# One ring, one list: replacing groups and pools by a single ordered list of operations for all engines

## Chip, cores, metric

One core of one Trainium2 chip, the other cores idle. The time is device microseconds of one execution. The profile's span is shorter than the time reported, by 1.7 to 2.2 us (3.0 and 2.9 in two executions of run 14). Engines: PE multiplies matrices, DVE is the vector engine, ACT the one for Ln and Exp, POOL is GpSimd; SBUF is the on-chip memory that holds the rows, PSUM the one that PE writes, in banks. All runs quoted are of the fast state; ratios are the mean time of one kernel's fast runs over that of the kernel before in the same rounds on the same chip, so not quite the ratio of the medians quoted. The kernel before was 174.5 to 175.4 us by chip and round.

## The reference

```python
x = np.abs(np.random.randn(32, 512, 1024)).astype(np.float32) + 1e-6
return np.sum(1.0 / x, axis=-1).astype(np.float32)
```

16384 rows of 1024 numbers lie as 128 partitions of 128 rows; "row" below means one row on all 128 partitions, 0.524 MB. There is no divide: with a and b the two halves of a row, 1/a + 1/b = (a + b) / (ab). So a product ab (512 wide), Ln, Exp(-x) for 1/(ab), and a multiply with a sum over the row.

## The kernel before

```python
A, B, C = (2, 0, GP, False), (2, 0, GP, True), (1, 1, GP, False)
GROUPS = ([A, B, A, B, C, B, A, B] * 7 + [A, B, A, B, A]
          + [(1, 0, GP, True), (1, 0, GP, False)] * 2 + [(1, 0, GP, True), (1, 0, DV, True)])
# xpool 16 buffers, ppool 4, rpool and spool (PSUM) 2 each
for np_, ns, eng, on_pe in GROUPS:
    xt = xpool.tile([P, n, D], f32, tag="xt")
    nc.sync.dma_start(out=xt, in_=x_v[:, c0 : c0 + n, :])        # mostly 2 rows, 1 MB
    eng.tensor_tensor(out=pr, in0=xt[:, :np_, :H], in1=xt[:, :np_, H:], op=mult)  # POOL
    if on_pe:   # a + b on PE: two matmuls with the identity into one PSUM bank
        for j in range(np_):
            for h in range(2):
                nc.tensor.matmul(sm[:, j, :], lhsT=ident, rhs=xt[:, j, h*H:(h+1)*H],
                                 start=h == 0, stop=h == 1)
    ...  # 7 rows go through ACT alone: Ln, Exp over the whole row
    nc.scalar.activation(out=pr, in_=pr, func=Ln, scale=S)
    nc.scalar.activation(out=rc, in_=pr, func=Exp, scale=-1.0)   # rc = pr, or PSUM
    ...  # DVE: "short" reduction rc * sm (512 wide), or "long" xt * rc (1024 wide)
```

## Time and profile before

| | before | changed |
|---|---|---|
| time, us | 174.56 | 179.68 |
| span of the profiled run | 172.6 | 177.8 |
| loads | 67 | 34 |
| last load landed | 164.0 | 162.5 |
| last reduction ended | 169.8 | 175.2 |
| busy: PE / DVE / ACT / POOL | 121 / 110 / 142 / 143 | 148 / 139 / 131 / 117 |

Landing minus start is transfer; last reduction minus last landing is what the engines still owe when the input is complete. The views are in the prediction.

### The profile page before, as it was taken

Reading aid. Unit: us, or ns where it says so; the run is one execution under the profiler, and the core shown is the slowest. Engines: PE = TensorE matmul, PEld = TensorE weight load, DVE = VectorE, ACT = ScalarE, POOL = GpSimd, SP = SyncE. Lnnn points to the kernel's source line nnn. Section 1 sums busy time; section 2 is a strip of 40 time slices with the busy share of each in tenths; the row PEclk is TensorE's granted clock in tenths of the full one; section 3 lists DMA queues with packets and bytes.
Section 4 is the critical chain, followed back from the end, with each engine's and each line's share of the span. In section 5 each row is a group of like instructions: output and inputs, shape, how many; then the busy total and the mean of one; then the engine's idle time right before and its main releaser. Section 6 shows DMA issues by size and latency. Waiting matters only on the chain.

```text
span 172.6 us, 1342 instructions
## 1 busy us (share of the span) xinstructions
PE 120.9 (70%) x256; PEld 47.4 (27%) x256; DVE 109.8 (64%) x243; ACT 142.0 (82%) x156; POOL 143.4 (83%) x72
## 2 busy tenths in 40 slices
PE   0099776767876767788666668977667876669480
PEld 0043322222332222233322223422222332223130
DVE  0009757874776757775578847468576755787791
ACT  2159989899878998889888996889988898988981
POOL 1599699969989799987999688997999979999920
PEclk9999999999999999999999996999999999999999
DMA  5999999999999999999999999999999999999500
GB/s 190 416 433 425 423 420 423 421 421 423 418 425 420 423 418 423 423 420 423 421 421 420 423 414 423 421 420 420 425 418 425 425 420 421 421 412 408 220 0 15
DMA packets 9799, 67.25 MB, mean 390 GB/s; under 512 B 1088, under 2 KB 1216, under 8 KB 1984
## 3 DMA queue, kind: packets, MB, share of 16 engines
q1 hardware_dynamic: 9792, 67.18, 94.0%
q8 instruction: 2, 0.03, 0.1%
q14 instruction: 5, 0.04, 0.1%
HBM read 67.11 MB, written 0.07 MB: 389 GB/s over the span
## 4 chain that ended last, share of the span: by engine, by line
DMA 78%; POOL 11%; ACT 2%; issue 2%; DVE 2%; SPq 1%; PE 1%; POOLq 0%; DVEq 0%
DMA xt<-in_x_dram 78%; POOL pr L85 11%; SPq L83 1%; ACT pr L106 1%; PE sm L90 1%; DVE xt L118 1%; ACT rc L111 1%; DVE pr L118 0%; ACT pr L111 0%; DVE pr L85 0%; POOLq L85 0%; DVE sums L118 0%; DVEq L118 0%; DVEq L157 0%
## 5 line engine op out<-in xcount | busy, mean ns | idle before, releaser
L85 POOL TENSOR_TENSOR pr<-xt 128x1024 f32<-128x1024 f32 (+1 forms) x66 | 142.7, 2166 | 21.1 <-DMA xt<-in_x_dram 15.2
L90 PE MATMUL sm<-xt,ident 128*128 128x512 f32 x256 | 120.9, 617 | 47.0 <-DMA xt<-in_x_dram 45.0
L118 DVE CUSTOM_DVE_ANT_1 xt<-xt,rc 128x1024 f32<-128x1024 f32 x57 | 67.7, 1219 | 50.2 <-issue 27.2
L106 ACT ACTIVATE pr<-pr 128x1024 f32<-128x1024 f32 (+1 forms) x67 | 65.0, 970 | 24.5 <-POOL pr L85 23.7
L90 PEld LDWEIGHTS sm<-xt,ident 128*128 128x128 f32 x256 | 47.4, 195 | 119.7 <-issue 57.8
L118 DVE CUSTOM_DVE_ANT_0 pr<-pr,sm 128x512 f32<-128x512 f32 x64 | 41.6, 685 | 9.8 <-ACT pr L111 8.6
L111 ACT ACTIVATE pr<-pr 128x1024 f32<-128x1024 f32 (+1 forms) x34 | 34.2, 1006 | 1.0
L111 ACT ACTIVATE rc<-pr 128x1024 f32<-128x1024 f32 (+1 forms) x33 | 29.9, 906 | 0.8
L118 DVE DVE_READ_ACCUMULATOR2_ANT sums<- 128x1 f32 x121 | 10.0, 82 | 0.0
L99 ACT ACTIVATE xt<-xt 128x1024 f32<-128x1024 f32 x7 | 7.3, 1041 | 0.0
L98 ACT ACTIVATE xt<-xt 128x1024 f32<-128x1024 f32 x7 | 7.3, 1040 | 0.0
L55 ACT ACT_TABLE_LOAD x1 | 1.3, 1283 | 0.7 <-PEq L146 0.7
L99 ACT ACTIVATION_READ_ACCUMULATOR xt<-xt 128x1 f32 x7 | 1.3, 186 | 0.0
L85 DVE TENSOR_TENSOR pr<-xt 128x512 f32<-128x512 f32 x1 | 0.7, 689 | 0.0
masks.py:197 POOL MEMSET ident<- 128x128 f32 x1 | 0.2, 204 | 0.3 <-POOLq L146 0.3
masks.py:199 POOL TENSOR_SCALAR_AFFINE_SELECT ident<-ident 128x128 f32<-128x128 f32 x1 | 0.3, 292 | 0.1
L146 POOL MEMSET const-float32-0.0<- 128x1 f32 x1 | 0.1, 98 | 0.2 <-issue 0.2
L146 POOL MEMSET const-bfloat16-1.0<- 128x1 bf16 x1 | 0.1, 101 | 0.0
L146 POOL MEMSET const-uint8-127<- 128x1 uint8 x1 | 0.1, 101 | 0.0
L146 POOL MEMSET const-float32-1.0<- 128x1 f32 x1 | 0.1, 98 | 0.0
## 6 DMA issues: line engine op xcount, KB each, us to landing
xt<-in_x_dram SPq DMA_DIRECT2D x61, 1024.0 KB, 19.8
xt<-in_x_dram SPq DMA_DIRECT2D x6, 512.0 KB, 15.6
out_dram<-sums SPq DMA_DIRECT2D x1, 64.0 KB, 1.5
```

The source lines that it names most:

```text
L55: nc.scalar.add_instruction(mybir.InstLoadActFuncSet(name=nc.get_next_instruction_name(), act_func_set_id=act_sets.index("natural_log_exp_ ...
L83: nc.sync.dma_start(out=xt, in_=x_v[:, c0 : c0 + n, :])
L85: eng.tensor_tensor(out=pr, in0=xt[:, :np_, :H], in1=xt[:, :np_, H:], op=mult)
L90: nc.tensor.matmul(sm[:, j, :], lhsT=ident, rhs=xt[:, j, h * H : (h + 1) * H], start=h == 0, stop=h == 1,)
L98: nc.scalar.activation(out=xt[:, j, :], in_=xt[:, j, :], func=Ln)
L99: nc.scalar.activation(out=xt[:, j, :], in_=xt[:, j, :], func=Exp, scale=-1.0, accum_out=sums[:, c0 + j : c0 + j + 1],)
L106: nc.scalar.activation(out=pr, in_=pr, func=Ln, scale=S)
L111: nc.scalar.activation(out=rc, in_=pr, func=Exp, scale=-1.0)
L118: nc.vector.tensor_tensor_reduce(out=row, in0=row, in1=rec, scale=S, scalar=0.0, op0=mult, op1=add, accum_out=sums[:, c0 + j : c0 + j + 1],)
L146: nc = _bacc.Bacc("TRN2", target_bir_lowering=False, num_devices=1)
```

## The change

Its intent: fewer, larger loads from one ring of 40 rows; less work for POOL and ACT; all engines' orders and all buffer slots chosen together in one list. `P` is a product on POOL, `S` the sum a + b on PE, `L` and `E` Ln and Exp, `R` a reduction on DVE (short if the row has an S), `D` a load. `+2` means two rows, `@` names the product slot (L) or the PSUM bank (C, S, E). New are `C` + `V`, a copy of b to PSUM by a matmul and the product on DVE from it, and `W`, the product on DVE with both halves in SBUF. Dependences between engines are still waited for; only the order is fixed.

```diff
-    A, B, C = (2, 0, GP, False), (2, 0, GP, True), (1, 1, GP, False)
-    GROUPS = ( ... )
+    R = 40      # ring
+    NP = 22     # product slots
+    PLAN = """
+        D8 D8 D8 D8 D8 P0+2 C3@7 S2@0 V3 L0+2@0 P2 S3@1 E0+2@6 P4+2 S6@2 L2+2@2 R0 E2+2 R1
+        ...
+        E38+2 R37 D7 C43@6 P47 V44 C46@7 V43 C41@5 R38 L47@0 P45 V46 E47 S42@0 V41
+        ...
+        P121 L119+2@0 R118 S121@1 E119+2@6 W122 R117 L121+2@2 P123 S122@2 R119 E121+2 W124
+        ...
+        L126@14 S127@1 E126 R125 L127@4 R126 E127 R127
+    """.split()
...
+            elif op == "C":
+                nc.tensor.matmul(ps[:, b, :], lhsT=ident, rhs=xs(r, 1), start=True, stop=True)
+            elif op in "WV":
+                in1 = xs(r, 1) if op == "W" else ps[:, copied[r], :]
+                nc.vector.tensor_tensor(out=prod[:, p, :], in0=xs(r, 0), in1=in1, op=mult)
```

The list has 73 P (93 rows), 20 C + V, 15 W, 71 S, 128 R, 70 L and 70 E.

More of the change, by code (lines that the diff above doesn't have):

```diff
@@ L31 @@
     F = 128
+    R = 40
+    NP = 22
     S = float(2**17)
-    GP, DV = nc.gpsimd, nc.vector
-    A, B, C = (2, 0, GP, False), (2, 0, GP, True), (1, 1, GP, False)
-    GROUPS = (
-        [A, B, A, B, C, B, A, B] * 7
-        + [A, B, A, B, A]
-        + [(1, 0, GP, True), (1, 0, GP, False)] * 2
-        + [(1, 0, GP, True), (1, 0, DV, True)]
-    )
+    PLAN = """
+        D8 D8 D8 D8 D8 P0+2 C3@7 S2@0 V3 L0+2@0 P2 S3@1 E0+2@6 P4+2 S6@2 L2+2@2 R0 E2+2 R1
+        S7@3 P6+2 L4+2@4 R2 R3 E4+2@6 L6+2@6 R4 P8+2 C11@5 E6+2 R5 D8 S10@0 V11 R6 L8+2@8
+        P10 S11@1 R7 E8+2@6 P12+2 S14@2 L10+2@10 R8 E10+2 R9 S15@3 P14+2 L12+2@12 R10 R11
+        E12+2@6 L14+2@14 R12 P16+2 C19@5 E14+2 R13 D8 S18@0 V19 R14 L16+2@16 P18 S19@1 R15
+        E16+2@6 P20+2 S22@2 L18+2@18 R16 E18+2 R17 S23@3 P22+2 L20+2@20 R18 R19 E20+2@6
+        L22+2@0 R20 D5 P24+2 C27@5 E22+2 R21 S26@0 V27 R22 L24+2@2 P26 S27@1 R23 E24+2@6
+        P28+2 S30@2 L26+2@4 R24 E26+2 R25 D6 S31@3 P30+2 L28+2@6 R26 R27 E28+2@6 L30+2@8 R28
+        E30+2 R29 P32+2 C35@5 S34@0 V35 R30 R31 L32+2@10 P34 S35@1 E32+2@6 P36+2 S38@2
+        L34+2@12 R32 D6 E34+2 R33 S39@3 P38+2 L36+2@14 R34 R35 E36+2@6 L38+2@16 R36 P42
+        C44@5 E38+2 R37 D7 C43@6 P47 V44 C46@7 V43 C41@5 R38 L47@0 P45 V46 E47 S42@0 V41
+        L46@1 P40 R39 L42+4@18 S43@1 E46 S44@2 E42+4 S45@3 L40+2@2 R42 R43 P55 E40+2 C53@7
+        R44 R45 P50 C49@6 V53 S47@0 V49 L53@9 P51 E53 W48 S41@1 P54 R47 L48+2@10 S40@0 D5
+        E48+2@6 R41 P52 L54+2@4 R49 P60 S57@1 L50+3@6 R40 W56 S56@0 P57 R48 E54+2@4 L60@12
+        R55 P59 S46@2 D4 L56+2@13 R54 P58 E50+3@5 S53@3 R46 P65 L58+2@15 R52 C61@4 E56+2 W62
+        S63@2 P63+2 R51 E60@7 V61 S64@6 R57 L61+2@20 R56 P66 L63+3@17 R60 S65@0 R53 L66@0
+        R50 D4 D3 S66@1 E61+2@3 P67 E66 R61 E63+3 S68@5 P72 R66 R62 P69 L72@2 S70@1 E72@7
+        R65 E58+2@3 P70 R63 S69@0 R64 W68 W71 L67+2@10 S67@2 R58 D3 L69+3@3 R59 D3 D2 D3 D2
+        S71@3 D3 P74 E67+2 R72 E69+3 P79 C75@6 R67 R68 C78@7 L79@6 P77 V75 S73@2 L74@1 V78
+        E79 W73 D2 L78@7 P76 R70 S74@4 E74 R71 E78@7 R69 L75+3@12 R78 S79@1 P80 R74 L73@8
+        C81@7 P82 E75+3@4 R79 C84@3 V81 P83 L80@9 R75 D2 S80@0 E73 V84 E80 S83@1 R76 D1
+        L81+4@15 P87 R80 P88 S85@3 R77 D2 D1 D1 E81+4 W85 S84@0 P86 R73 L85@0 R83 E85 S82@1
+        P89+2 L86+2@20 R85 R84 E86+2@6 C92@5 R82 L88+3@2 P91 R86 S81@0 D1 D1 D1 D1 D1 D1 V92
+        P93 E88+3@2 C95@6 R87 D1 S93@1 L91+3@5 W94 V95 R90 S91@5 L94+2@10 P96 R81 E91+3 R88
+        S92@0 P97+2 L96@19 R91 E94+2@6 R93 R92 E96@5 C99@4 P101 R94 L97+2@12 S101@0 V99 P100
+        E97+2@1 R95 S103@4 L99@1 P102 R97 L100+2@8 P103 S100@6 R96 L102@14 E100+2 R98 L103@0
+        P105 C104@7 R89 E102@5 S105@1 E103 P106 V104 E99@2 R102 L104+2@20 S106@3 P108 R99
+        L106@2 E104+2 P107 S108@5 R103 E106 R105 L107@3 R106 S107@1 E107 W111 W109 L111@4
+        W110 E111@7 S109@2 R107 L108+3@15 P112+2 R111 S104@1 E108+3 R101 R100 S110@0 P114+2
+        L112+2@10 R109 R104 E112+2@6 R108 S115@1 R110 L114+2@5 P116 R112 S114@0 E114+2 W118
+        W117 L116@18 R115 P119 S118@2 L117+2@12 R114 E116@6 R113 P120 E117+2 S117@0 R116
+        P121 L119+2@0 R118 S121@1 E119+2@6 W122 R117 L121+2@2 P123 S122@2 R119 E121+2 W124
+        R120 L123+2@7 P125 S125@0 R122 E123+2@5 R121 P126 L125@19 R124 S126@2 E125 P127 R123
+        L126@14 S127@1 E126 R125 L127@4 R126 E127 R127
@@ L62 @@
     )
-    xpool = ctx.enter_context(tc.tile_pool(name="xpool", bufs=16))
-    ppool = ctx.enter_context(tc.tile_pool(name="ppool", bufs=4))
-    opool = ctx.enter_context(tc.tile_pool(name="opool", bufs=1))
-    rpool = ctx.enter_context(
-        tc.tile_pool(name="rpool", bufs=2, space=bass.MemoryType.PSUM)
-    )
-    spool = ctx.enter_context(
-        tc.tile_pool(name="spool", bufs=2, space=bass.MemoryType.PSUM)
-    )
-    sums = opool.tile([P, F], f32)
-    ident = opool.tile([P, P], f32)
@@ L77 @@
-    make_identity(nc, ident)
-    c0 = 0
-    for np_, ns, eng, on_pe in GROUPS:
-        n = np_ + ns
-        xt = xpool.tile([P, n, D], f32, tag="xt")
-        nc.sync.dma_start(out=xt, in_=x_v[:, c0 : c0 + n, :])
-        pr = ppool.tile([P, np_, H], f32, tag="pr")
-        eng.tensor_tensor(out=pr, in0=xt[:, :np_, :H], in1=xt[:, :np_, H:], op=mult)
-        if on_pe:
-            sm = spool.tile([P, np_, H], f32, tag="sm")
-            for j in range(np_):
+    pool = ctx.enter_context(tc.tile_pool(name="pool", bufs=1))
@@ new lines, with parse @@
+    pspool = ctx.enter_context(
+        tc.tile_pool(name="pspool", bufs=1, space=bass.MemoryType.PSUM)
+    )
+    ring = pool.tile([P, R, D], f32)
+    prod = pool.tile([P, NP, H], f32)
+    sums = pool.tile([P, F], f32)
+    ident = pool.tile([P, P], f32)
+    ps = pspool.tile([P, 8, H], f32)
+    make_identity(nc, ident)
+    def parse(tok):
+        body, _, b = tok[1:].partition("@")
+        r, _, n = body.partition("+")
+        return tok[0], int(r), int(n or 1), int(b) if b else None
@@ new lines, with xs @@
+    ops = [parse(tok) for tok in PLAN]
+    pslot = {r + j: b + j for op, r, n, b in ops if op == "L" for j in range(n)}
+    def xs(r, h):
+        return ring[:, r % R, h * H : (h + 1) * H]
+    loaded = 0
+    bank, copied, halves = {}, {}, set()
+    with tc.manual_schedule():
+        for op, r, n, b in ops:
+            p = pslot.get(r)
+            if op == "D":
+                n, r = r, loaded
+                while n:
+                    a = r % R
+                    m = min(n, R - a)
+                    nc.sync.dma_start(
+                        out=ring[:, a : a + m, :], in_=x_v[:, r : r + m, :]
+                    )
+                    r, n = r + m, n - m
+                loaded = r
+            elif op == "P":
+                while n:
+                    a, p = r % R, pslot[r]
+                    m = min(n, R - a)
+                    nc.gpsimd.tensor_tensor(
+                        out=prod[:, p : p + m, :],
+                        in0=ring[:, a : a + m, :H],
+                        in1=ring[:, a : a + m, H:],
+                        op=mult,
+                    )
+                    r, n = r + m, n - m
+            elif op == "C":
+                copied[r] = b
+                nc.tensor.matmul(
+                    ps[:, b, :], lhsT=ident, rhs=xs(r, 1), start=True, stop=True
+                )
+            elif op in "WV":
+                in1 = xs(r, 1) if op == "W" else ps[:, copied[r], :]
+                nc.vector.tensor_tensor(
+                    out=prod[:, p, :], in0=xs(r, 0), in1=in1, op=mult
+                )
+            elif op == "S":
+                bank[r] = b
+                halves.add(r)
@@ L89 @@
                 for h in range(2):
                     nc.tensor.matmul(
-                        sm[:, j, :],
+                        ps[:, b, :],
                         lhsT=ident,
-                        rhs=xt[:, j, h * H : (h + 1) * H],
+                        rhs=xs(r, h),
                         start=h == 0,
@@ L96 @@
                     )
-        for j in range(np_, n):
-            nc.scalar.activation(out=xt[:, j, :], in_=xt[:, j, :], func=Ln)
-            nc.scalar.activation(
-                out=xt[:, j, :],
-                in_=xt[:, j, :],
-                func=Exp,
-                scale=-1.0,
-                accum_out=sums[:, c0 + j : c0 + j + 1],
-            )
-        nc.scalar.activation(out=pr, in_=pr, func=Ln, scale=S)
-        if on_pe:
-            rc = pr
-        else:
-            rc = rpool.tile([P, np_, H], f32, tag="rc")
@@ L111 @@
-        nc.scalar.activation(out=rc, in_=pr, func=Exp, scale=-1.0)
-        for j in range(np_):
-            if on_pe:
-                row, rec = rc[:, j, :], sm[:, j, :]
-            else:
-                row = xt[:, j, :].rearrange("p (h e) -> p h e", h=2)
-                rec = rc[:, j, :].unsqueeze(1).to_broadcast([P, 2, H])
-            nc.vector.tensor_tensor_reduce(
-                out=row,
-                in0=row,
-                in1=rec,
-                scale=S,
-                scalar=0.0,
-                op0=mult,
-                op1=add,
-                accum_out=sums[:, c0 + j : c0 + j + 1],
-            )
@@ L128 @@
-        c0 += n
-    assert c0 == F, c0
-    nc.sync.dma_start(out=out_v, in_=sums)
+            elif op == "L":
+                pg = prod[:, p : p + n, :]
+                nc.scalar.activation(out=pg, in_=pg, func=Ln, scale=S)
+            elif op == "E":
+                pg = prod[:, p : p + n, :]
+                rc = pg
+                if b is not None:
+                    rc = ps[:, b : b + n, :]
+                    for j in range(n):
+                        bank[r + j] = b + j
+                nc.scalar.activation(out=rc, in_=pg, func=Exp, scale=-1.0)
+            elif op == "R":
+                other = ps[:, bank[r], :]
+                if r in halves:
+                    row = prod[:, p, :]
+                else:
+                    row = ring[:, r % R, :].rearrange("p (h e) -> p h e", h=2)
+                    other = other.unsqueeze(1).to_broadcast([P, 2, H])
+                nc.vector.tensor_tensor_reduce(
+                    out=row,
+                    in0=row,
+                    in1=other,
+                    scale=S,
+                    scalar=0.0,
+                    op0=mult,
+                    op1=add,
+                    accum_out=sums[:, r : r + 1],
+                )
+            elif op == "X":
+                row = ring[:, r % R, :]
+                nc.scalar.activation(out=row, in_=row, func=Ln)
+                nc.scalar.activation(
+                    out=row,
+                    in_=row,
+                    func=Exp,
+                    scale=-1.0,
+                    accum_out=sums[:, r : r + 1],
+                )
@@ L135 @@
+        nc.sync.dma_start(out=out_v, in_=sums)
 _INS = ['x']
```

## The prediction

> **What bounds the kernel now.** I read the page's slices first, then the loads by their time of issue, the traffic in short windows round the end, the chain, and last the single instructions of each engine. First the slices and the queue:
>
> ```profile
> span 172.6 us, 1342 instructions
> ...
> DMA  5999999999999999999999999999999999999500
> GB/s 190 416 433 425 423 420 423 421 421 423 418 425 420 423 418 423 423 420 423 421 421 420 423 414 423 421 420 420 425 418 425 425 420 421 421 412 408 220 0 15
> ```
>
> The DMA engines never pause from slice 0 to slice 37: the input is a stream at 421 GB/s (412 and 408 where the last six loads of one row run), so 67.11 MB take some 159.5 us. A slice is 4.315 us; 0.82 MB in the first puts the start of the stream at about 2.4 us. When does it end? The last load by its time of issue, and the traffic in windows:
>
> ```profile
> L83 SPq DMA_DIRECT2D xt<-in_x_dram x1: 328/328/328, 151.5 to 151.5; - x1
> DMA to landing us min/median/max: 12.5/12.5/12.5
> ```
> ```profile
> 161.50:162.50 1.00, 0.83 (x2) 0.00 (x0) 1.00 (x3) 0.97 (x3) 1.00 (x1) 1.00 0.39 156
> 162.50:163.50 1.00, 0.00 (x0) 0.00 (x0) 1.00 (x3) 0.97 (x3) 1.00 (x2) 1.00 0.12 49
> ```
>
> The last load was issued at 151.5 and landed 12.5 us later, at 164.0. The second fence says why not at 162: the last two columns (DMA share, GB/s) fall to 0.12 and 49, so some two of the 16 DMA engines run about 2 us behind the rest. A row is there only when the slowest has delivered. After 164.0 the kernel still needs 8.6 us to the end of its span. The chain names the same two stages, and between them a stretch where POOL had fallen behind (its eight products in a row from 139 to 159 us):
>
> ```profile
> DMA 78%; POOL 11%; ACT 2%; issue 2%; DVE 2%; SPq 1%; PE 1%; POOLq 0%; DVEq 0%
> ```
>
> So today's 172.6 is: 2.4 to start, 161.6 of stream to its slowest engine, 8.6 of tail; and the reported 174.53 is 1.93 above the span. A gain must come from a faster stream or a shorter tail. Compute between counts only if it ends later than the stream.
>
> **What the Trainium skill says.** (1) "DMA: Bandwidth & Descriptors", section "Where 436 GB/s comes from", puts the ceiling at 435 GB/s; its section on the iDMA fabric gives 408.7 GB/s for 1 MiB loads in 4 KiB rows. The trace agrees: 408 to 412 with 4 KB runs (one row), 421 with 8 KB runs (two rows), so longer runs come nearer to the ceiling. (2) The same page, "Why a DMA increments its semaphore by 16 and not by 1": a DMA is complete only when every engine has delivered. That is the straggler above. (3) "SBUF — State Buffer", "Who interferes with whom": a VectorE instruction with two SBUF inputs contends with a GpSimd instruction that reads SBUF, one waiting for the whole of the other; with one input in PSUM it does not. The trace before cannot show it: its one such product on DVE ran at 167.04 us, after POOL had ended at 165.06.
>
> **The change, part by part.**
>
> *Loads.* 67 loads (61 of two rows, 6 of one) become 34: seven of 8 rows, then 5 to 7, 4 to 2, and ten of one. Per load cost, from the two rates: one row, 0.5243 MB at 410, takes 1.279 us; two rows, 1.0486 MB at 421.3, take 2.489 us. Twice the first less the second is 0.069 us, a fixed cost per load, whose number of runs (128) does not depend on its rows. Assuming it stays so for 32 KB runs, 33 fewer loads save 33 x 0.069 = 2.3 us, and the last landing goes from 164.0 to 161.7. An estimate, and the term I trust least.
>
> *Does the ring starve the stream?* Five loads of 8 rows are issued at once, 40 x 1.245 = 50 us of stream. The sixth needs R5: first rows at 2.4 + 8 x 1.245 = 12.4, three POOL products (2.4, 1.3, 2.4), two activations (1.0 each), two reductions (1.14 each): about 23 us, with 29 us of stream still queued. Later the six last loads stand in the list near row 92, so over 20 rows are queued. It never starves.
>
> *Start.* The first load now lands at about 12.5 where the first of before landed at 5.5, so compute begins 7 us later. It has to be made up by shorter work.
>
> *Work.* Counted from the list: POOL 20 products of two rows and 53 of one; DVE 20 products with one input in PSUM, 15 with both in SBUF, 71 short reductions and 57 long; ACT 140 activations with no single-row path left (it had 7 rows); PE 162 matmuls for 256. The durations are in the groups by form:
>
> ```profile
> L85 POOL TENSOR_TENSOR pr<-xt 128x1024 f32<-128x1024 f32 x54 | 127.6, 2365 | 20.3 <-DMA xt<-in_x_dram 15.0 <-ACT pr L106 1.1
> L118 DVE CUSTOM_DVE_ANT_1 xt<-xt,rc 128x1024 f32<-128x1024 f32 x57 | 67.7, 1219 | 50.2 <-issue 27.2 <-ACT rc L111 12.9 <-POOL pr L85 10.0
> L118 DVE CUSTOM_DVE_ANT_0 pr<-pr,sm 128x512 f32<-128x512 f32 x64 | 41.6, 685 | 9.8 <-ACT pr L111 8.6
> L85 POOL TENSOR_TENSOR pr<-xt 128x512 f32<-128x512 f32 x12 | 15.1, 1273 | 0.7 <-DMA xt<-in_x_dram 0.2
> ```
>
> POOL: 20 x 2.365 + 53 x 1.273 = 114.8 us, down from 142.7. DVE instructions overlap their neighbours, so I take starts, not durations:
>
> ```profile
> 66.89 1.22 DVE L118 CUSTOM_DVE_ANT_1 xt<-xt,rc 128x1024 f32<-128x1024 f32 x1
> 68.03 0.08 DVE L118 DVE_READ_ACCUMULATOR2_ANT sums<- 128x1 f32 x1
> 68.23 0.69 DVE L118 CUSTOM_DVE_ANT_0 pr<-pr,sm 128x512 f32<-128x512 f32 x1
> 68.85 0.08 DVE L118 DVE_READ_ACCUMULATOR2_ANT sums<- 128x1 f32 x1
> 68.85 0.68 DVE L118 CUSTOM_DVE_ANT_0 pr<-pr,sm 128x512 f32<-128x512 f32 x1
> ```
>
> A long reduction occupies 1.14 us, a short one or a product 0.61: 57 x 1.14 + (71 + 35) x 0.61 = 129.6 us. ACT likewise from starts: a Ln and Exp pair of one row 0.64 + 0.54 = 1.18, of two rows 1.08 + 0.95 = 2.03, so 0.85 per row more. With 23, 38, 7 and 2 pairs of one to four rows: 27.1 + 77.1 + 20.2 + 7.5 = 132 us. PE: 162 x 0.43 = 70. Each is under the 149 us from 12.5 to the last landing, so all can catch up, ACT and DVE with some 15 us of slack in total.
>
> *Tail.* Before, two-row groups, PSUM waits and the last row's product queued on DVE made 8.6 us. After: product on POOL 1.28, Ln 0.64, Exp 0.66, reduction and its read 0.69 plus gaps, 3.4 us after landing; the store and the end took 2.8 us before (reduction ended at 169.78, span at 172.6) and stay. So 6.2 us instead of 8.6, 2.4 us less.
>
> *Can the engines keep to it?* Rows 109 to 111 land at 2.4 + 112 x 1.245 = 141.8. From W111 on, DVE has 7 products, 16 short and 8 long reductions: 23 x 0.61 + 8 x 1.14 = 23.2, so DVE ends no sooner than 165.0, where the tail says 161.7 + 3.4 = 165.1. The list is balanced to the last microsecond; there is no reserve at the end for a wait it did not foresee.
>
> *Sum.* 161.7 + 6.2 + 1.93 = 169.8. For waits the list did not foresee I add 1.0 us, a judgement: seven of the 15 DVE products with two SBUF inputs stand in the last 20 us, each can meet a POOL product, and 0.3 to 0.6 us each would be 2 to 4 us, part of it hidden. That gives **170.8 us**.
>
> **Rivals.** *A: the rate does not move* (32 KB runs cost as much per byte, or the two slow DMA engines are slow for another reason). Landing stays at 164.0, engines then have 2 us of reserve: 164.0 + 6.2 + 1.93 = 172.1, 1.4% faster. For it: in the slices equal loads vary between 414 and 433 GB/s, as much as the effect. Against it: the step from 410 to 421 with the run length. *B: DVE or ACT becomes the bound at the end*, through two-input products that meet POOL, or a product slot or PSUM bank not free at the list's time, in strictly ordered queues. For it: the balance just worked out and the 22 slots; before, 23 waits of DVE on issue alone were 27 us. Against: ACT and DVE still have 10% spare over the whole. It would add 2 to 4 us to the sum: 172 to 174. *C: the late start is not made up*, so work trails the stream by microseconds throughout: 7 us later at the start, but ACT needs 1.03 us per row where the stream brings one each 1.245, so it catches up by the middle unless starved by whole loads landing at once. If it did not, 175 and more.
>
> **Range and chances.** The faster side is limited: 169.8 with no unforeseen wait, perhaps 169 if the stragglers shrink as well. The slower side holds A and B alone (172 to 173) and rarely both or C (174 and more). 2% faster is 171.04, close to my centre, so faster and same are near even: 0.50 and 0.46, slower 0.04. Range 169.0 to 173.6.
>
> **What would show it.** Right: GB/s of 427 or more in the slices of the 8-row loads; the last load landing near 161.7; POOL, DVE busy near 115 and 150 (busy sums count overlap); under 4 us from the last landing to the last reduction. Wrong: 421 in those slices and landing at 164 (rival A); DVE products with two SBUF inputs well over 0.7 us or POOL products that stretch beside them, and DVE without gaps to the end (B); engines idle on landings late while rows queue up early (C). A slice with DMA under 9 before the end would refute the ring argument.

## The result

The changed kernel took 179.68 us (179.57 to 179.87) against 174.56: ratio 1.028, interval 1.025 to 1.031. It is slower by 2.8%, outside the predicted range of 169.0 to 173.6.

The page's slices of the changed kernel:

```profile
span 177.8 us, 1426 instructions
...
DMA  6999999999999999999999999999999999990000
GB/s 221 428 413 457 428 413 457 428 413 457 422 420 450 424 422 418 427 438 431 437 454 413 414 415 429 431 415 437 409 421 436 417 414 411 410 366 21 0 0 15
```

The stream never pauses and is faster: the slices of the big loads (the first 15 full ones) swing between 413 and 457 with a mean of 430, where the prediction's sign was 427 or more. A single slice can lie above the 435 that the prediction cites; the mean does not. The last load, by its time of issue:

```profile
L121 SPq DMA_DIRECT2D ring<-in_x_dram x1: 327/327/327, 151.5 to 151.5; - x1
DMA to landing us min/median/max: 11.0/11.0/11.0
```

It landed at 162.5, 1.5 us sooner than before. But the last instruction of DVE's timeline ends 12.7 us later:

```profile
175.12 0.08 DVE L176 DVE_READ_ACCUMULATOR2_ANT sums<- 128x1 f32 x1
```

So the loss is between landing and last reduction. The page's busy times were 117 us for POOL and 139 for DVE, where the prediction's signs were 115 and 150. Busy time by engine in stretches of 20 us (columns: stretch and its length, then busy us of PE, PE's weight loads, DVE, ACT, POOL, clock, DMA share, GB/s) shows who had no time left:

```profile
60.00:80.00 20.00, 17.29 (x37) 7.35 (x36) 12.56 (x29) 13.86 (x16) 12.82 (x11) 0.91 0.99 422
80.00:100.00 20.00, 19.90 (x47) 8.57 (x46) 19.07 (x40) 16.87 (x19) 15.43 (x11) 1.00 1.00 430
100.00:120.00 20.00, 20.00 (x48) 8.82 (x47) 19.55 (x44) 17.21 (x19) 14.92 (x11) 1.00 1.00 424
120.00:140.00 20.00, 18.08 (x42) 7.36 (x41) 19.23 (x38) 17.24 (x20) 16.92 (x13) 1.00 1.01 423
140.00:160.00 20.00, 17.72 (x37) 7.28 (x37) 18.87 (x39) 14.79 (x19) 12.68 (x9) 0.91 1.00 404
160.00:180.00 20.00, 13.73 (x31) 5.35 (x29) 15.20 (x34) 12.17 (x15) 3.09 (x3) 0.93 0.03 8
```

From 80 us on DVE is full (15.20 us is all there is from 160 to its end at 175.2) and PE nearly so, while POOL, the busiest engine before, has room. The groups by form say what filled DVE and PE:

```profile
L151 PE MATMUL ps<-ring,ident 128*128 128x512 f32 x284 | 128.3, 604 | 4.8 <-DVE sums L176 4.4
L130 POOL TENSOR_TENSOR prod<-ring 128x512 f32<-128x512 f32 x53 | 69.7, 1338 | 23.1 <-DMA ring<-in_x_dram 22.0 <-DVE prod L144 1.0
L144 DVE TENSOR_TENSOR prod<-ring 128x512 f32<-128x512 f32 x15 | 16.9, 1149 | 0.0
L144 DVE TENSOR_TENSOR prod<-ring,ps 128x512 f32<-128x512 f32 x20 | 13.6, 683 | 18.3 <-PE ps L139 18.3
```

Two things. The products with both inputs in SBUF took 1149 ns on average where those with one in PSUM took 683. And PE has 284 + 40 = 324 records, where the list has 71 x 2 + 20 = 162 matmuls: each shows as two records, 0.43 us apart. A piece of the chain of waits has 28 of them in 12.02 us (the experiments' expectations call a record a pass):

```profile
77.22 12.02 PE ps L151 x28
```

One W in the timeline, with the POOL products it ran beside:

```profile
118.17 5.29 POOL L130 TENSOR_TENSOR prod<-ring 128x1024 f32<-128x1024 f32 x3 [1.22 <-ACT prod L160]
118.92 2.17 DVE L144 TENSOR_TENSOR prod<-ring 128x512 f32<-128x512 f32 x1
```

POOL began first, and the DVE product took 2.17 us. Not every W is like this: eight took 679 to 735 ns, seven 850 to 2469. All seven began while a POOL product was running; of the eight only one did (735 ns). The excess over 683 ns is 7.0 us in all, 6.9 of it after 80 us and 3.6 in the seven last.

The stalls reach PE too. PE is at work almost without a gap from 63 to 121 us. Then it stands still for 0.98, 0.81 and 2.18 us, each time just after a long W and until a DVE reduction has ended. The longest, and the three W before it:

```profile
147.00 4.75 DVE L144 TENSOR_TENSOR prod<-ring 128x512 f32<-128x512 f32 x3
152.41 17.62 PE L151 MATMUL ps<-ring,ident 128*128 128x512 f32 x36 [2.18 <-DVE sums L176]
```

The chain of waits of the changed kernel, however, puts PE first:

```profile
PE 38%; DMA 29%; DVE 16%; ACT 9%; issue 6%; POOL 1%; DVEq 0%; SPq 0%; ACTq 0%
```

So theories for the experiments: **stalls** (DVE's W behind POOL), **PE** (twice the work that I had counted), and **whole loads** (rows come late, in lumps of eight).

### The profile page after: what moved, and what is told of

The parts are those of the page before. It is cut to its first block, busy times and chain, and to the rows that moved or that the text cites. A ratio compares the mean times of both kernels' runs of the same rounds, so it can differ in the third digit from the quotient of the medians.

```text
span 177.8 us, 1426 instructions
## 1 busy us (share of the span) xinstructions
PE 147.5 (83%) x324; PEld 62.0 (35%) x324; DVE 138.9 (78%) x291; ACT 130.8 (74%) x141; POOL 117.0 (66%) x79
## 4 chain that ended last, share of the span: by engine, by line
PE 38%; DMA 29%; DVE 16%; ACT 9%; issue 6%; POOL 1%; DVEq 0%; SPq 0%; ACTq 0%
PE ps L151 32%; DMA ring<-in_x_dram 29%; DVE ring L176 7%; PE ps L139 6%; DVE prod L144 6%; ACT prod L160 5%; DVE prod L176 3%; ACT ps L168 2%; ACT prod L168 2%; POOL prod L130 1%; DVE sums L176 1%; SPq L121 0%; ACTq L160 0%; DVEq L144 0%; DVEq L176 0%
## 5 line engine op out<-in xcount | busy, mean ns | idle before, releaser
L130 POOL TENSOR_TENSOR prod<-ring 128x512 f32<-128x512 f32 (+1 forms) x73 | 116.3, 1621 | 46.4 <-DMA ring<-in_x_dram 43.9
L151 PE MATMUL ps<-ring,ident 128*128 128x512 f32 x284 | 128.3, 604 | 4.8 <-DVE sums L176 4.4
L160 ACT ACTIVATE prod<-prod 128x1024 f32<-128x1024 f32 (+3 forms) x70 | 67.0, 973 | 40.0 <-POOL prod L130 22.6
L151 PEld LDWEIGHTS ps<-ring,ident 128*128 128x128 f32 x284 | 54.1, 193 | 77.6 <-issue 60.3
L176 DVE CUSTOM_DVE_ANT_1 ring<-ring,ps 128x1024 f32<-128x1024 f32 x57 | 67.7, 1215 | 10.3 <-ACT ps L168 10.3
L176 DVE CUSTOM_DVE_ANT_0 prod<-prod,ps 128x512 f32<-128x512 f32 x71 | 46.3, 681 | 7.6 <-ACT prod L168 3.4
L139 PE MATMUL ps<-ring,ident 128*128 128x512 f32 x40 | 22.7, 679 | 21.9 <-DMA ring<-in_x_dram 21.9
L168 ACT ACTIVATE prod<-prod 128x1024 f32<-128x1024 f32 (+3 forms) x39 | 37.5, 973 | 0.7
L168 ACT ACTIVATE ps<-prod 128x1024 f32<-128x1024 f32 (+2 forms) x31 | 29.5, 955 | 2.2 <-DVE sums L176 1.5
L144 DVE TENSOR_TENSOR prod<-ring,ps 128x512 f32<-128x512 f32 x20 | 13.6, 683 | 18.3 <-PE ps L139 18.3
L139 PEld LDWEIGHTS ps<-ring,ident 128*128 128x128 f32 x40 | 7.9, 210 | 33.8 <-issue 20.2
L144 DVE TENSOR_TENSOR prod<-ring 128x512 f32<-128x512 f32 x15 | 16.9, 1149 | 0.0
```

The source lines that it names most:

```text
L130: nc.gpsimd.tensor_tensor(out=prod[:, p : p + m, :], in0=ring[:, a : a + m, :H], in1=ring[:, a : a + m, H:], op=mult,)
L139: nc.tensor.matmul(ps[:, b, :], lhsT=ident, rhs=xs(r, 1), start=True, stop=True)
L144: nc.vector.tensor_tensor(out=prod[:, p, :], in0=xs(r, 0), in1=in1, op=mult)
L151: nc.tensor.matmul(ps[:, b, :], lhsT=ident, rhs=xs(r, h), start=h == 0, stop=h == 1,)
L160: nc.scalar.activation(out=pg, in_=pg, func=Ln, scale=S)
L168: nc.scalar.activation(out=rc, in_=pg, func=Exp, scale=-1.0)
```

## The experiments

Fourteen kernels; four runs of each. Times are medians, ratios to the kernel before. The labels number them. All but the second, sixth and eighth gave correct results.

### 1. No product with two SBUF inputs

```diff
- W48 ... W124   (15 of them, DVE)
+ P48 ... P124   (POOL)
```

> The 15 DVE products with both inputs in SBUF go to POOL at the same place of the list; all else as in the changed kernel (179.7 us). Theory PE (each fp32 matmul of 512 columns is two passes, so the PE work is 139 us and not 70, and PE is the bound from 63 us on): PE work is the same 324 passes; only the stalls of DVE that hold PSUM banks back go, so 1 to 3 us faster, not back to 174.5. Theory contention (DVE stands behind POOL, 1149 ns a product where 683 is free): DVE loses 15 x 1.15 = 17 us of work, POOL rises from 117 to about 136, and the time falls by 5 us or more, to 174 or less. Profile: no DVE product over 0.7 us, POOL products of one row back near 1273 ns.

Measured 172.0 us, ratio 0.983: 7.7 us faster than the changed kernel and 1.7% faster than before. That is the stall theory's size, though PE's records are the same 324. POOL's single products went back near their old duration although there are 15 more:

```profile
L129 POOL TENSOR_TENSOR prod<-ring 128x512 f32<-128x512 f32 x68 | 84.8, 1289 | 13.9 <-DMA ring<-in_x_dram 13.7
```

Work also went from DVE to POOL here (15 x 0.61 us even without stalls), so runs 8 and 10 try to separate that.

### 2. Half of each sum on PE

```diff
- for h in range(2): matmul(ps[:, b, :], rhs=xs(r, h), start=h == 0, stop=h == 1)
+ matmul(ps[:, b, :], rhs=xs(r, 0), start=True, stop=True)
```

> Wrong result on purpose: each sum of two halves on PE is left at its first half, so 71 x 2 = 142 of the 324 matmul passes go; DVE, ACT, POOL, the loads and the list are as in the changed kernel. Theory PE: PE work falls from 139 to about 78 us, PE leaves the chain, and the time falls by 5 us or more, to 171 to 175, with what is left set by DVE and its two-input products. Theory contention: PE had slack, under 1.5 us faster.

Measured 175.9 us, ratio 1.005: 3.8 us faster than the changed kernel, between the two expectations. PE's doubled work costs, but less than the stalls; DVE's products still take 1150 ns. The granted clock was lower here (0.89 to 0.91, in the changed kernel 0.98 to 0.99), so PE's busy time fell from 147.5 to 104.0 us only; runs 6 and 8 are alike (0.87 to 0.94).

### 3. First load split

```diff
- D8 D8 D8 D8 D8 P0+2
+ D2 D2 D2 D2 D8 D8 D8 D8 P0+2
```

> Only the first load of 8 rows is made four of 2, so that the engines can start at about 5.6 us and not 13.5. Theory late start: 4 to 7 us faster. Theory PE with whole loads: nothing, within 1 us, because up to 63 us every engine waits for the next whole load of 8 rows to land, and the row that opens the saturated stretch (row 48, landing with row 55 at 63.2) comes no earlier.

Measured 178.8 us, ratio 1.023: 0.85 us faster. An early start alone is worth little, as expected.

### 4. Loads of two rows everywhere

```diff
- D8 / D7 / ... / D3
+ D2 D2 D2 D2 / ... / D2 D1
```

> Every load is cut into loads of at most 2 rows at the same place of the list (67 or so loads and not 34). The stream term of the prediction says 0.069 us more per load, so the last landing moves from about 161.6 to about 164. Theory PE with whole loads: rows 48 and up reach PE up to 8 us sooner, PE gets its 139 us of work done by about the end of the stream in spite of the slower stream, so the time falls by 3 to 6 us. Theory stream (the gain of the change is in the big loads, and giving them up costs): 2 us slower, 182. If neither PE nor loads matter but contention does: within 1 us.

Measured 173.5 us, ratio 0.992: 6.2 us faster, although the last landing moved to 165.6 (73 loads):

```profile
L121 SPq DMA_DIRECT2D ring<-in_x_dram x1: 328/328/328, 155.5 to 155.5; - x1
DMA to landing us min/median/max: 10.1/10.1/10.1
```

```profile
169.34 0.08 DVE L176 DVE_READ_ACCUMULATOR2_ANT sums<- 128x1 f32 x1
```

The last reduction ends 3.8 us after that, where the prediction had 3.4. Fed two rows at a time the engines follow the stream in spite of W and of PE. So the big loads gave the stream 3.1 us against this run and cost the engines 12.7 - 3.8 = 8.9. That is not the lumps alone: with the other timing W took 944 ns on average, so the stalls fell from 7.0 to 3.9 us as well.

### 5. Runs 1 and 4 together

```diff
- W48 ... , D8 ...
+ P48 ... , D2 D2 D2 D2 ...
```

> The edits of the first and the fourth run together: no DVE product with two SBUF inputs (172.0 us alone) and loads of at most 2 rows (173.5 alone). Theory stream floor: the small loads put the last landing at about 164.9, and 164.9 plus the tail of 3.4 + 2.8 and the 1.9 outside the span is 173; the fourth run is there already, so 172.5 to 173.5, no gain over it and slower than the first run. Theory engines: both edits only take waits away from engines, so they add up, to 168 or less.

Measured 174.4 us, ratio 0.999. The gains don't add; it is 0.9 us slower than run 4 (on another chip; 0.7% by the ratios). POOL, with the W's products, is then at work to 167.3 without a gap over its last four products.

### 6. Runs 1 and 2 together

```diff
- W48 ... ; two matmuls per sum
+ P48 ... ; one matmul per sum
```

> Wrong result on purpose: the first and second runs' edits together, so neither the stalls behind POOL nor the second half of the PE work that the prediction had left out, with the loads of the changed kernel. If these two are what the prediction got wrong, the rest of its sum should hold: last landing 161.7, 169.8 with no unforeseen wait, so 169.3 to 170.6. If the late start matters beside them, or if a third cause is left, 171 or more. In the profile PE should have gaps after 80 us where the first run has none.

Measured 171.9 us, ratio 0.984: the same as run 1. The expectation of 169.3 to 170.6 was missed. With the stalls gone, 142 PE records less (busy 103.3 us, in run 1 143.1) gain nothing. In the timelines of both runs POOL works without a gap from 157.4 to 164.8, and the ends of both are alike to 0.02 us:

```profile
157.36 7.48 POOL L129 TENSOR_TENSOR prod<-ring 128x512 f32<-128x512 f32 x6
```

```profile
157.40 7.44 POOL L129 TENSOR_TENSOR prod<-ring 128x512 f32<-128x512 f32 x6
```

(first of run 1, then of run 6). POOL's queue, made longer by this very edit, may hold the end there; no run relieves POOL and PE at once, so that is not shown.

### 7. Loads of four at first, no W

```diff
- D8 D8 D8 D8 D8 ... D8 ... D8
+ D2 D2 D4 D4 D4 ... (rows 0 to 55), and P for W
```

> The first run's edit, and the seven loads of 8 rows made 2, 2, 4 and twelve of 4, with the small loads of the end as in the changed kernel. Seven to eight loads more cost 0.5 us of stream (landing near 162.2), and PE is fed earlier, so that it enters row 56 with less behind it. Theory PE fed by whole loads: PE ends with the stream and the time is 162.2 + 6.2 + 1.9, so 170 to 171. Theory that the first run's rest is not PE: 172, unchanged.

Measured 172.1 us, ratio 0.986: as run 1. Lumps no longer matter once the stalls are gone; the theory that PE's late feeding holds run 1 falls.

### 8. W fed from copies, half sums

```diff
- W48                    (both inputs in SBUF)
+ C48@4 ... V48          (second input in PSUM), 15 times; and one matmul per sum
```

> Wrong result on purpose: sums on PE halved as in the second run (175.9 us), and the 15 products with two SBUF inputs are made products with one input in PSUM, fed by 15 more copies on PE, so they stay on DVE, POOL gets no work more, and only what DVE reads them from is changed. Theory contention: the four us between the second run and the sum of the prediction are the stalls, and POOL's extra work is what held the first and sixth runs at 172, so 169.5 to 171. Theory that merely moving DVE work off DVE helped in the first run: DVE has the same instructions here, so 175 or more.

Measured 173.7 us (one of four 172.2), ratio 0.992: 2.2 us faster than run 2, with the same DVE instructions and nothing more for POOL. All 35 products now take 685 ns. The sign is the stall theory's, the size is not: I had expected 169.5 to 171. DVE, without gaps over the last 10 us, ends it at 169.4.

### 9. A list of my own, and 10. the same with two SBUF inputs

Nine repeats the pattern of rows 8 to 39 to row 119; ten replaces its 17 C + V by W:

```diff
- P8+2 C11@5 E6+2 R5 D8 S10@0 V11 R6 ...
+ P8+2       E6+2 R5 D8 S10@0 W11 R6 ...
```

> A list of my own: the pattern of eight rows that the changed kernel's list has for rows 8 to 39 repeated to row 119 (per eight rows POOL 8.4 us, PE 7.7 us counted with two passes, ACT 8.1, DVE 7.6, against 9.96 of stream), no product with two SBUF inputs, 26 loads (2, 2, 4, then 8, at the end 6 to 1), single rows at the end. Every engine has 15% to spare in every stretch. If what was wrong is stalls and lopsided stretches, it runs right behind the stream: landing near 161.2, plus 6.2 and 1.9, so 169.3 to 170.5, faster than both kernels. If a cause is left that I have not named: 172 or more.

> The ninth run with its 17 products on DVE given both inputs in SBUF, without the copies, so PE gets lighter by 15 us and nothing else changes. Theory contention: each of them waits for POOL products, in the profile well over 0.7 us each and POOL's beside them longer; in the middle there is room to hide it, at the end it adds, so 1 to 4 us slower than the ninth. Without contention: equal or faster, PE being lighter.

Measured 173.2 (ratio 0.992) and 175.2 us (1.003). Nine missed its 169.3 to 170.5; ten is 2.0 us slower than nine, with PE relieved of 17 copies. The groups of nine, then of ten:

```profile
L127 POOL TENSOR_TENSOR prod<-ring 128x512 f32<-128x512 f32 x19 | 24.2, 1276 | 0.1
L141 DVE TENSOR_TENSOR prod<-ring,ps 128x512 f32<-128x512 f32 x17 | 11.6, 684 | 15.6 <-PE ps L136 15.6
```

```profile
L126 POOL TENSOR_TENSOR prod<-ring 128x512 f32<-128x512 f32 x19 | 30.0, 1588 | 0.1
L140 DVE TENSOR_TENSOR prod<-ring 128x512 f32<-128x512 f32 x17 | 25.8, 1516 | 10.6 <-DMA ring<-in_x_dram 10.6
```

This is the cleanest pair for the stalls: only where DVE reads its second input from (and the copies, and the granted clock, 0.93 against 0.96 to 0.98) differ. DVE's product rises from 684 to 1516 ns, and POOL's single products beside it from 1276 to 1588. Of these 14.2 + 5.8 us of busy time 2 reach the end, presumably because this list has spare time in most stretches.

### 11 and 12. My list with finer loads

```diff
- D8 (eight times from row 40 on)
+ D4 D4          (11);   12: D4 from row 4 on, D3 D2 at the end, D1 x8
```

> The ninth run (173.2 us) with its eight loads of 8 rows from row 40 on made sixteen of 4; the list is the same. In the ninth run the stream ended near 160.9 but POOL had no gap from 140 on and ended at 163.1, ACT and DVE behind it, 7.8 us from the last landing to the last reduction. Theory that whole loads of 8 leave every engine a backlog that it carries into the end: eight loads more cost 0.55 us of stream, rows come up to 5 us earlier, so 170 to 171.5. Theory that the ninth is bound by its last list entries themselves: 173 or more.

> The same list with loads of 4 from row 4 on and of 3, 2 and eight of 1 at the end, 43 loads: 1.2 us more of stream than the ninth run, so landing near 162.1, and the end fed row by row. Theory of the carried backlog: 170 to 171.5 like the eleventh, the slower stream taking back what the finer end gives. If single rows at the end are what is missing, 169.5 to 170.5.

Measured 173.9 (ratio 0.994) and 173.35 us (0.991): no gain. The backlog theory was missed in both (170 to 171.5), and so was 169.5 to 170.5 in 12; 11 met its other theory, 173 or more. So a backlog from large loads does not hold my list's end; that its own entries do is argued: in 9 and 11 DVE still has three long reductions to do, one after another, from 164 us on.

### 13 and 14. Is it POOL's end, is PE near its bound?

```diff
- P122 ... P124                 (run 1)
+ C122@3 ... V122, C124@4 ... V124      (13: DVE from copies)
- all 15 W                      (changed kernel, full sums)
+ C + V for all 15              (14)
```

> The first run (172.0 us), with rows 122 and 124 alone multiplied on DVE from a copy in PSUM instead of on POOL: POOL has two products of 1.3 us less in its last ten us, PE two copies of 0.86 us more. In the first run POOL had no gap from 157.4 to 164.8. Theory POOL's end: 170.5 to 171.5. Theory PE is the bound of the first run after all: 173 or more, since PE had no gap from 80 to 165 us there.

> The changed kernel with correct result, all 15 products with two SBUF inputs fed from a copy in PSUM, so no stalls, POOL at 114 us and PE at 139 + 13 = 152 us of passes. Theory stalls only: 173 to 175, as in the eighth run (173.7), which had half the sums. Theory PE near its bound: PE begins at 13.6, has gaps of some 8 us to 63 us, so it cannot end before 13.6 + 152 + 8 = 174, and the time is 178 or more.

Thirteen: 173.1 us, ratio 0.990, 0.6% slower than run 1 by their ratios (the intervals just overlap; one execution took 174.8). So relieving POOL gained nothing, and the PE expectation (173 or more) was just met: POOL ends at 164.0, but the last reduction now waits for PE:

```profile
167.87 0.69 DVE L175 CUSTOM_DVE_ANT_0 prod<-prod,ps 128x512 f32<-128x512 f32 x1 [0.35 <-PE ps L150]
```

Fourteen: 184.5 us, ratio 1.050. Every stall is gone (all 35 products take 684 ns), yet 30 PE records more make it 4.8 us slower than the changed kernel (on another chip; 3.8 by the ratios). PE is now the bound, with no gap from 63 us to its end at 178:

```profile
PE 158.5 (87%) x354; PEld 67.9 (37%) x354; DVE 133.4 (73%) x291; ACT 130.9 (72%) x141; POOL 113.7 (63%) x79
```

## Why the prediction was wrong

- **The stream: mechanism right, size short.** 33 fewer loads were to move the landing from 164.0 to 161.7; it came to 162.5, so 0.045 us per load saved and not 0.069. The price per load is not what was short: with one list, 34 loads land at 162.5 and 73 (run 4) at 165.6, which is 0.08 per load. Why the kernel before lands as early as 164.0 with 67 loads is open. Rival A, no gain, is refuted. The ring never starved, as said.
- **The tail after landing: somewhat short.** 3.4 us was predicted. Run 4 comes nearest with 3.8; runs 1, 5, 6 and 7, free of stalls, show 4.9 to 5.0.
- **The step that failed is "for waits the list did not foresee I add 1.0 us".** Landing to last reduction took 12.7 us, not 3.4 + 1.0. With 0.8 of later landing and 8.3 here, less 0.2 us at the end of the span, the miss of 8.9 us is accounted for.
- **Its larger part is rival B, named and under-sized.** I priced a W at 0.3 to 0.6 us. The mean excess was 1149 - 683 = 0.47 us: the price per instruction was right. The seven near the end came to 2 to 4 us by this price and to 3.6 in the trace, but the sum has only 1.0 of it ("part of it hidden"). The eight before them, another 3.4 us, were not counted at all; the prediction only has "15 us of slack in total" (its own sums against 149 us give 17 for ACT and 19 for DVE). DVE is full from 80 us on, so 15 x 0.47 = 7.0 us of stall had nowhere to go; taking W away gave 7.7. That is not the stalls alone, for run 1 takes 9.2 us of work off DVE too. Where the instructions stay on DVE, in runs 8 and 10, the stalls alone were worth 2.2 and 2.0 us. How the 7.7 splits between stalls and the lighter load of DVE is not settled: run 8 keeps DVE's work and, with PE halved, still ends at 173.7 where run 6 ends at 171.9. Of B's other part, a product slot not free in time, the trace shows little: POOL waited for ACT's use of a slot once, 1.2 us.
- **"PE: 162 x 0.43 = 70" was a plain error.** 0.43 us is one record, and a matmul has two; the page of before showed 256 records, where its program has 128 matmuls (64 rows x 2). The work is 324 x 0.43 = 139 us, and PE stood in none of my rivals. Rows 40 to 47 alone carry eight sums and four copies, 8 x 1.72 + 4 x 0.86 = 17.2 us, where the stream brings eight rows in 10. Halving the sums gave 3.8 us with the stalls and nothing without them; adding 30 records (and leaving the products on DVE) cost 12.5 us against run 1 (11.7 by the ratios). So PE has no room left, but removing PE work alone doesn't repair the kernel.
- **The granted clock is not the cause.** The profiled execution of the changed kernel had 0.978, the three others 0.989 to 0.990, and they took as long (179.66 to 179.87 against 179.57); run 1 took 171.98 at 1.000 and 172.01 at 0.987.
- **Rival C, the late start, is half right.** Compute began at 13.54 us where before it began at 5.58, 8.0 later and not 7. "ACT needs 1.03 us per row where the stream brings one each 1.245, so it catches up by the middle" left out DVE and PE, which did not. The late start alone is worth 0.85 us (run 3); late lumps throughout cost 6.2 net of a 3.1 us slower stream (run 4), but nothing measurable without stalls (run 7). Runs 1, 2 and 4 gain 7.7, 3.8 and 6.2 but don't add. My reading is that the three causes share one delay, each taking reserve that the others then need; it is not tested further.
- **Open:** why no correct list came under 172. In run 1 POOL and PE end within about a microsecond of each other, and relieving either (6, 13) gained nothing; both at once was not tried. My own lists were held by their ends. Run 1 is the fastest found: 1.7% under the kernel before, 4.3% under the changed one (172.0 against 179.7).

## What to carry to other kernels

A list balanced so that several engines end together has no reserve, so price a contended instruction by the slack of its engine in that stretch, never by the average over the span. Check an engine's work by dividing the profile's record count by the program's instruction count before multiplying anything. Larger loads buy stream time and can charge every consumer for waiting on the last row of the lump: compare both in the same units before choosing.

## What the Trainium skill lacked or had wrong

- "SBUF — State Buffer", section "Who interferes with whom": its rule that a VectorE instruction with two SBUF inputs contends with GpSimd's reads is confirmed, but it gives no size for this pair. Here a 128x512 fp32 product took 679 to 2469 ns, 1149 or 1516 on average against 684 with one input in PSUM, and POOL's own product rose from 1276 to 1588.
- "FP8 and Floating Point Precision", section "TensorE Precision Notes", says that true FP32 takes four passes through the array, which would have warned me. It does not say how a trace shows this: here as two records 0.43 us apart per matmul (324 records for 162 matmuls), 0.86 us in all for 512 columns.
- "DMA: Bandwidth & Descriptors", section "Latency and other measured facts", guesses that slow DMA engines have to do with loads issued from GpSimd; here all loads come from the sync engine, and a few engines still trail by about 2 us at the end (in the changed kernel the DMA share is 0.17 to 0.06 from 160 to 162 us; the trace does not say which engines). The last row waits for them, and no page gives a figure for this.
